# Two of four convolution blocks on GpSimd and ScalarE, and the threshold search's update on ScalarE

## The chip, the cores and the metric

The kernel runs on one core of a Trainium2 chip. A core has five engines with a queue of instructions each, worked off in order: TensorE (PE: matmuls, with weight loads as PEld), VectorE (DVE), ScalarE (ACT), GpSimd (POOL) and SyncE (SP, which issues the DMAs). They meet in two memories, SBUF and PSUM, and wait for one another through semaphores. The metric is the device time of one execution, in microseconds (us).

## The reference, cut to what matters

Two layers of a first block (`DEPTH = 2`), then a second block (a gated recurrence and an MLP), which the change doesn't touch. A layer of the first block, for 1024 tokens:

```python
p = h @ w_in[l]
u_val, u_gate, g_conv, c_q, c_kv, k_idx, w_idx, g_attn = jnp.split(p, offsets, axis=-1)
# conformer_conv: 512 channels, 31 taps, causal, depthwise
a = u_val * jax.nn.sigmoid(u_gate)
y = conv(a, conv_w) + conv_b
y_conv = (silu(layernorm(y, ln_g, ln_b)) @ w_pw2) * silu(g_conv)
# dsa_attention, for each block of 128 queries
score = einsum("bth,bths->bts", w_b, relu(einsum("bthd,bsd->bths", qi_b, k_idx)))
score = where(causal, score, -inf)
_, sel = lax.top_k(score, 256)
# ... attention over the selected keys, gated by silu(g_attn)
y = concatenate([y_conv, y_attn], -1) @ w_out[l]
x = x + gate * rmsnorm(y, g_post[l])
```

## The kernel before, in words

SBUF is cut into pages of 1024 float32 a partition; a buffer is a page (`pg`) or a list of pages. Products on TensorE are made from operands that are split in a high and a low part: ScalarE copies the high part (helper `split`, L264), VectorE subtracts it (L265). A scheduler orders the instructions of each engine at build time; the program gives it generators that yield after each unit of work, `weave` interleaves them by rates, and `prior` puts a generator's instructions forward or back in that order. At run time every queue is in order.

A layer's stages around the change, with their generators: `g_inputs` makes the convolution's four input blocks A[0] to A[3] (128 channels each by 1024 positions, even positions in the first half of a page, odd ones in the second; VectorE's L673 writes the halves). `g_latents` makes the latents of queries and keys (L801 on VectorE is their norm). `g_scores` runs over query blocks 2 to 4, then 5 to 7: matmuls L852, ScalarE's relu L854, VectorE's weighted sum L857 and L859, and at the end of each block GpSimd's causal mask L862 (`affine_select`). `g_gates` makes eight gate blocks on TensorE, evacuated by ScalarE (L689), with a weight split for each. `g_topk` finds, per query, the 256th largest score, bit by bit in two stages (15 and 16 bits): `top1` for query blocks 2 (VectorE, L921) and 3, 4 (ScalarE, L913), `top2` for 5, 6 (VectorE) and 7 (ScalarE). It begins with ScalarE's L893, which counts the scores above zero. For a ScalarE block, each bit is a count (a Sign with an accumulated sum), then three GpSimd operations on a column of 128 numbers (L916, L917, L919) that move the threshold `half`, which the next count reads.

`g_conv` computes the convolution of a block with three filters of half the length: a sum of the halves (L710), a scaled copy on ScalarE (L711), 15 + 30 + 2 = 47 fused taps on VectorE (L703: product with a column of weights plus the running sum, on 497 to 512 columns), and two copies of 15 columns (L726). It runs in the background of inputs, latents, scores and gates at priority -30, `top1` at -200. The layer norm of the four results (`g_norm_conv`) comes behind the search and the attention's preparation. Attention begins behind `top1`.

## Time and profile before

| | |
|---|---|
| runs before | 3029.22 and 3030.83 us, median 3030.02 |
| the profiled execution (span) | 3029.3 us |
| PE busy | 2906.8 us, 96% |
| DVE busy | 2229.9 us, 74% |
| ACT busy | 1679.8 us, 55% |
| POOL busy | 247.2 us, 8% |
| mean granted TensorE clock | 0.983 |

The profiled execution lasts 0.7 us less than the median. An engine's busy share is an average over the whole span. The page's part 2 cuts the span in 40 slices of 75.7 us and gives each engine's share there in tenths; PEclk is the granted TensorE clock (1.00 is the upper of its two levels, 2.4 GHz; a figure between is a mix with the lower, 1.2 GHz). Layer 0's conv inputs, latents and search lie in slices 2 to 6, layer 1's in slices 10 to 15. Every row read from it stands in its own section below.

### The profile page before, as it was taken

Reading aid. Unit: us, or ns where it says so; the run is one execution under the profiler, and the core shown is the slowest. Engines: PE = TensorE matmul, PEld = TensorE weight load, DVE = VectorE, ACT = ScalarE, POOL = GpSimd, SP = SyncE. Lnnn points to the kernel's source line nnn. Section 1 sums busy time; section 2 is a strip of 40 time slices with the busy share of each in tenths; the row PEclk is TensorE's granted clock in tenths of the full one; section 3 lists DMA queues with packets and bytes.
Section 4 is the critical chain, followed back from the end, with each engine's and each line's share of the span. In section 5 each row is a group of like instructions: output and inputs, shape, how many; then the busy total and the mean of one; then the engine's idle time right before and its main releaser. Section 6 shows DMA issues by size and latency. Waiting matters only on the chain.

```text
span 3029.3 us, 40735 instructions
## 1 busy us (share of the span) xinstructions
PE 2906.8 (96%) x15235; PEld 2362.8 (78%) x15235; DVE 2229.9 (74%) x4118; ACT 1679.8 (55%) x3032; POOL 247.2 (8%) x630
## 2 busy tenths in 40 slices
PE   9998787999999888999999999999999999999999
PEld 6877565778877665777888888888888888888887
DVE  5998899776988899756555667656666587776875
ACT  6248766737147866646444466555555654454454
POOL 0005511000005511000000000000000000000000
PEclk9999989999999989999999999999999999999999
DMA  8222102154101200133122211101013344456443
GB/s 276 63 40 63 42 18 77 48 193 149 39 18 42 63 19 18 36 112 118 49 62 62 79 35 36 56 29 56 29 37 122 103 143 153 151 201 238 153 146 111
DMA packets 218637, 264.14 MB, mean 87 GB/s; under 512 B 11504, under 2 KB 153543, under 8 KB 218439
## 3 DMA queue, kind: packets, MB, share of 16 engines
q1 hardware_dynamic: 218438, 261.54, 26.7%
q8 instruction: 119, 1.95, 0.3%
q14 instruction: 80, 0.65, 0.1%
HBM read 201.21 MB, written 60.29 MB: 86 GB/s over the span
## 4 chain that ended last, share of the span: by engine, by line
PE 58%; DVE 5%; POOL 2%; ACT 2%; DMA 1%; issue 1%; POOLq 0%; ACTq 0%
PE ps L269 15%; PE ps L271 15%; PE ps L270 15%; PE ps L331 5%; PE ps L1499 2%; DVE pg L921 2%; POOL consts L917 1%; PE ps L1164 1%; PE ps L1154 1%; POOL consts L919 1%; POOL consts L916 1%; DMA pg<-in_w_in_dram 1%; PE ps L1488 0%; DVE pg L1130 0%; PE ps L498 0%
## 5 line engine op out<-in xcount | busy, mean ns | idle before, releaser
L269 PE MATMUL ps<-pg,pg 128*128 128x512 f32 (+2 forms) x3080 | 1178.7, 384 | 15.1 <-DVE pg L265 4.2
L270 PE MATMUL ps<-pg,pg 128*128 128x512 f32 (+2 forms) x3080 | 1176.3, 383 | 0.0
L271 PE MATMUL ps<-pg,pg 128*128 128x512 f32 (+2 forms) x3080 | 1176.0, 382 | 0.0
L264 ACT ACTIVATE pg<-pg 128x512 fp32r<-128x512 f32 (+2 forms) x884 | 481.7, 591 | 527.7 <-PE ps L271 157.2
L269 PEld LDWEIGHTS ps<-pg,pg 128*128 128x128 f32 x3080 | 580.5, 189 | 132.9 <-DVE pg L265 10.1
L271 PEld LDWEIGHTS ps<-pg,pg 128*128 128x128 f32 x3080 | 580.6, 189 | 109.8 <-issue 3.7
L270 PEld LDWEIGHTS ps<-pg,pg 128*128 128x128 f32 x3080 | 580.8, 189 | 107.9 <-issue 3.5
L265 DVE TENSOR_TENSOR pg<-pg,pg 128x512 fp32r<-128x512 f32 (+2 forms) x884 | 528.2, 636 | 136.4 <-ACT pg L264 121.3
L278 POOL TENSOR_TENSOR consts<-consts 128x1 f32<-128x1 f32 x56 | 31.3, 559 | 2069.0 <-DVE consts L277 2069.0
L913 ACT ACTIVATE pg<-pg,consts 128x512 bf16<-128x512 uint16 (+5 forms) x186 | 166.8, 897 | 40.8 <-POOL consts L919 36.1
L703 DVE SCALAR_TENSOR_TENSOR pg<-pg,consts,pg 128x512 f32<-128x512 f32 (+15 forms) x256 | 176.9, 742 | 0.4
L331 PE MATMUL ps<-pg,pg 128*128 128x512 f32 x768 | 175.9, 389 | 0.0
L921 DVE TENSOR_SCALAR_CACHE_REDUCE pg<-pg,consts 128x384 bf16<-128x384 uint16 (+5 forms) x186 | 170.9, 919 | 2.3
L331 PEld LDWEIGHTS ps<-pg,pg 128*128 128x128 f32 x768 | 143.8, 188 | 29.6
L1138 ACT ACTIVATE pg<-pg,consts 128x256 f32<-128x256 f32 (+7 forms) x128 | 98.9, 774 | 70.2 <-DVE consts L1130 51.7
L1154 PE MATMUL ps<-consts,pg 128*128 128x128 f32 x576 | 107.7, 291 | 1.9 <-ACT pg L1160 1.1
L852 PE MATMUL ps<-pg,pg 128*128 128x512 f32 (+3 forms) x320 | 86.3, 370 | 14.7 <-DVE pg L844 9.4
L1164 PE MATMUL ps<-pg,pg 128*64 128x128 f32 x1152 | 92.5, 292 | 5.8 <-DVE pg L1147 1.7
L1116 PE MATMUL ps<-pg,pg 128*128 128x384 f32 (+5 forms) x192 | 79.4, 415 | 16.2 <-DVE consts L1130 7.9
L1160 ACT ACTIVATE pg<-ps 128x512 f32<-128x512 f32 (+1 forms) x112 | 57.8, 532 | 66.8 <-PE ps L1154 62.4
L917 POOL TENSOR_SCALAR consts<-consts 128x1 f32<-128x1 f32 x186 | 78.0, 419 | 179.1 <-ACT pg L913 173.5
L1164 PEld LDWEIGHTS ps<-pg,pg 128*64 128x64 f32 x1152 | 64.1, 141 | 35.1 <-issue 13.4
(350 smaller groups left out, 3810.7 us busy)
## 6 DMA issues: line engine op xcount, KB each, us to landing
pg<-in_w_in_dram SPq DMA_DIRECT2D x104, 512.0 KB
pg<-hidden SPq DMA_DIRECT2D x56, 512.0 KB
hidden<-pg SPq DMA_DIRECT2D x48, 512.0 KB
pg<-in_w_ada_dram SPq DMA_DIRECT2D x32, 512.0 KB
pg<-in_w_up_dram SPq DMA_DIRECT2D x32, 512.0 KB
pg<-in_w_down_dram SPq DMA_DIRECT2D x32, 512.0 KB
pg<-in_w_out_dram SPq DMA_DIRECT2D x24, 512.0 KB
x<-pg SPq DMA_DIRECT2D x24, 512.0 KB
```

What stands on the lines that cost most here:

```text
L264: self.nc.scalar.activation(hi, src, AF.Copy)
L265: self.nc.vector.tensor_sub(lo, src, hi.bitcast(F32))
L269: nc.tensor.matmul(ps, lhsT=wl, rhs=rh, start=first, stop=False)
L270: nc.tensor.matmul(ps, lhsT=wh, rhs=rl, start=False, stop=False)
L271: nc.tensor.matmul(ps, lhsT=wh, rhs=rh, start=False, stop=last)
L331: nc.tensor.matmul(ps, lhsT=w[z][k], rhs=act[y][k][:, a:b], start=k + n == 0, stop=3 * k + n == 3 * kt - 1)
L703: nc.vector.scalar_tensor_tensor(out, x[:, :512 - d], w, prev[:, d:], op0=OP.mult, op1=OP.add)
L913: nc.scalar.activation(junk_a(b), keys[b], AF.Sign, scale=-1.0, bias=col(tk["half"], b), accum_out=col(tk["cnt"], b))
L917: nc.gpsimd.tensor_scalar(col(tk["tm"], b), col(tk["cnt"], b), lim, -step, op0=OP.is_gt, op1=OP.mult)
L921: nc.vector.tensor_scalar(junk_d(b), keys[b], col(tk["cand"], b), None, op0=OP.is_ge, op1=OP.add, accum_out=col(tk["cnt"], b))
L1154: nc.tensor.transpose(pt[:, c:c + 128], Ps[hi][:, j * 128:j * 128 + 128], self.ident)
L1164: nc.tensor.matmul(uv[hi * 64:hi * 64 + 64], lhsT=V[j // 2][:, v:v + 64], rhs=th[:, jj * 256 + hi * 128:jj * 256 + hi * 128 + 128], start= ...
```

## The change

The blocks of the convolution are shared out: 0 and 1 stay on VectorE as fused taps, in one generator; 2 and 3 form a second one, `pconv`. For block 2 ScalarE makes each product into half a spare page (four halves in rotation) and GpSimd adds it to the running sum; for block 3 GpSimd makes the product too. Their first sum is on GpSimd as well. `pconv` has no priority offset; it runs along with the inputs and the latents and is drained before the scores are emitted. `Y` becomes a list that is filled by index.

In the search, ScalarE moves its own threshold: a Sign of the count plus a limit (`k2`, a column that VectorE presets), then an Identity that subtracts half a step times that sign. GpSimd has no part in the search any more. The start value and the limits are shifted to fit, and the column `hn` goes. All other lines of the diff remove comments.

```diff
+DVE_CONV, POOL_CONV = (0, 1), (2, 3)
...
-        A, Y, YA = [], [], []
+        A, Y, YA = [], [None] * 4, []
...
-        def g_conv():
+        def g_conv(blocks, split):
             cw, (g0, g1) = self.vec[f"conv_w{l}"], self.vec[f"conv_g{l}"]
-            add = nc.vector.tensor_add
+            add = nc.gpsimd.tensor_add if split else nc.vector.tensor_add
+            pp = self.pages(2) if split else []
+            prods = [pg[:, s] for pg in pp for s in halves]
 
             def tap(out, x, d, w, prev):
-                nc.vector.scalar_tensor_tensor(out, x[:, :512 - d], w, prev[:, d:], op0=OP.mult, op1=OP.add)
-            for j in range(4):
+                if split:
+                    q = self.ring("prods", prods)[:, :512 - d]
+                    if j == blocks[-1]:
+                        nc.gpsimd.tensor_scalar(q, x[:, :512 - d], w, None, op0=OP.mult)
+                    else:
+                        nc.scalar.activation(q, x[:, :512 - d], AF.Copy, scale=w)
+                    add(out, q, prev[:, d:])
+                else:
+                    nc.vector.scalar_tensor_tensor(out, x[:, :512 - d], w, prev[:, d:], op0=OP.mult, op1=OP.add)
+            for j in blocks:
...
                     for b in act:
                         nc.scalar.activation(junk_a(b), keys[b], AF.Sign, scale=-1.0, bias=col(tk["half"], b),
                                              accum_out=col(tk["cnt"], b))
-                        lim = col(tk["k2"], b) if limits else float(n_of[b] - 2 * TOPK)
-                        nc.gpsimd.tensor_scalar(col(tk["hn"], b), col(tk["half"], b), nxt, None, op0=OP.add)
-                        nc.gpsimd.tensor_scalar(col(tk["tm"], b), col(tk["cnt"], b), lim, -step, op0=OP.is_gt,
-                                                op1=OP.mult)
-                        nc.gpsimd.tensor_tensor(col(tk["half"], b), col(tk["tm"], b), col(tk["hn"], b), op=OP.add)
+                        nc.scalar.activation(col(tk["tm"], b), col(tk["cnt"], b), AF.Sign, bias=col(tk["k2"], b))
+                        nc.scalar.activation(col(tk["half"], b), col(tk["tm"], b), AF.Identity, scale=-0.5 * step,
+                                             bias=col(tk["half"], b))
...
-        conv = pr(g_conv(), 0)
+        conv, pconv = pr(g_conv(DVE_CONV, False), 0), g_conv(POOL_CONV, True)
...
-        weave((pr(g_inputs(), 11), 8), bg=[(more, RATES[l][8]), (conv, RATES[l][0])])
+        weave((pr(g_inputs(), 11), 8), bg=[(more, RATES[l][8]), (conv, RATES[l][0]), (pconv, 1.0)])
         drain(more)
         wq = idx_weights()
-        weave((pr(g_latents(), 9), 6), bg=[(conv, RATES[l][1])])
+        weave((pr(g_latents(), 9), 6), bg=[(conv, RATES[l][1]), (pconv, 6.0)])
+        drain(pconv)
```

The line numbers of the changed kernel are up to 14 higher: L862 is L875 there, L893 is L906, L913 is L928, L854 is L867, L264 is L265, L852 is L865. Its new lines are L710 (GpSimd's product), L712 (ScalarE's product), L713 (GpSimd's addition), L722 (the first sum), L930 and L931 (the threshold).

GpSimd's queue in layer 0, where the causal masks of the first score blocks stand. Before, they come first of all, and the search's columns follow:

```order
L278 TENSOR_TENSOR consts<-consts 128x1 x8
L862 AFFINE_SELECT pg_132_1342<-pg_132_1342 128x128
L862 AFFINE_SELECT pg_133_1343<-pg_133_1343 128x128
L862 AFFINE_SELECT pg_132_1342<-pg_132_1342 128x128
L916 TENSOR_SCALAR consts<-consts 128x1 x2
L917 TENSOR_SCALAR consts<-consts 128x1
L919 TENSOR_TENSOR consts<-consts 128x1
```

Now, the last rows of block 3's products and sums and what comes behind them (`pg_137`, `pg_138` hold the scores of query blocks 2 to 4, `pg_144` to `pg_146` those of 5 to 7):

```order
L710 TENSOR_SCALAR pg_69_582<-pg_95_833,consts 128x498 x2
L713 TENSOR_TENSOR pg_117_1149<-pg_69_582,pg_117_1149 128x498 x2
L710 TENSOR_SCALAR pg_68_581<-pg_95_833,consts 128x497 x2
L713 TENSOR_TENSOR pg_123_1380<-pg_68_581,pg_117_1149 128x497 x2
L875 AFFINE_SELECT pg_137_1520<-pg_137_1520 128x128
L875 AFFINE_SELECT pg_138_1521<-pg_138_1521 128x128
L875 AFFINE_SELECT pg_137_1520<-pg_137_1520 128x128
L875 AFFINE_SELECT pg_145_1817<-pg_145_1817 128x128
```

All 143 wide operations of the layer stand ahead of the first mask.

ScalarE's queue at the start of `top1`'s first stage in layer 0 (counts, relu of scores, gate evacuations and weight splits). Before:

```order
L893 ACTIVATE pg_146_1687,consts<-pg_132_1342,consts 128x640
L854 ACTIVATE pg_143_1670<-ps 128x1024
L689 ACTIVATE pg_152_1731<-ps 128x512
L913 ACTIVATE pg_146_1687,consts<-pg_148_1689,consts 128x512
L689 ACTIVATE pg_152_1731<-ps 128x512
L843 ACTIVATE pg_145_1672<-ps 128x384
L854 ACTIVATE pg_143_1670<-ps 128x896
L843 ACTIVATE pg_145_1672<-ps 128x384
L854 ACTIVATE pg_144_1671<-ps 128x896
L913 ACTIVATE pg_146_1687,consts<-pg_147_1688,consts 128x640
L854 ACTIVATE pg_144_1671<-ps 128x768
L913 ACTIVATE pg_146_1687,consts<-pg_148_1689,consts 128x512
```

Now:

```order
L867 ACTIVATE pg_148_1820<-ps 128x896
L906 ACTIVATE pg_150_1836,consts<-pg_137_1520,consts 128x640
L867 ACTIVATE pg_148_1820<-ps 128x768
L928 ACTIVATE pg_150_1836,consts<-pg_152_1838,consts 128x512
L930 ACTIVATE consts<-consts 128x1
L928 ACTIVATE pg_150_1836,consts<-pg_151_1837,consts 128x640
L931 ACTIVATE consts<-consts 128x1
L930 ACTIVATE consts<-consts 128x1
L928 ACTIVATE pg_150_1836,consts<-pg_152_1838,consts 128x512
```

From there all 30 counts of the stage and their 60 column operations follow one another without any other work; the next relu (L867) comes behind them, and eight rows further the split of the next gate weights, `L265 ACTIVATE pg_154_1873<-pg_153_1872 128x1024`. In layer 1 such a piece has 26 counts and 52 column operations.

TensorE's queue near that place in layer 0, the last score units and the gate product that needs these weights (`pg_154`, and `pg_155`, which VectorE's L266 makes from it):

```order
L865 MATMUL ps<-pg_109_1023,pg_149_1821 128x512 x2
L865 MATMUL ps<-pg_110_1024,pg_149_1821 128x512 x2
L865 MATMUL ps<-pg_109_1023,pg_149_1821 128x448 x2
L865 MATMUL ps<-pg_110_1024,pg_149_1821 128x448 x2
L270 MATMUL ps<-pg_42_288,pg_155_1874 128x512
L271 MATMUL ps<-pg_50_296,pg_154_1873 128x512
L272 MATMUL ps<-pg_42_288,pg_154_1873 128x512
```

The product's weights come from the split behind ScalarE's piece of counts.

## Rows read from the trace of the kernel before

**Rows 1.** The page, part 1: busy us, share and instructions of each engine.
```profile
PE 2906.8 (96%) x15235; PEld 2362.8 (78%) x15235; DVE 2229.9 (74%) x4118; ACT 1679.8 (55%) x3032; POOL 247.2 (8%) x630
```

**Rows 2.** Stretches: length, busy PE, PEld, DVE, ACT, POOL, granted clock, DMA share, GB/s.
```profile
111.00:232.00 121.00, 120.09 (x551) 97.43 (x549) 117.47 (x215) 44.77 (x77) 0.80 (x2) 1.00 0.21 40
232.00:354.00 122.00, 100.40 (x416) 78.57 (x416) 98.92 (x237) 96.12 (x196) 82.86 (x190) 0.93 0.19 58
354.00:400.00 46.00, 35.87 (x135) 25.04 (x134) 44.73 (x102) 38.04 (x69) 7.93 (x33) 0.93 0.08 25
...
925.00:1046.00 121.00, 105.07 (x441) 81.69 (x439) 104.95 (x259) 100.90 (x210) 84.00 (x190) 0.96 0.19 60
1046.00:1100.00 54.00, 46.49 (x197) 35.34 (x198) 51.67 (x128) 39.92 (x78) 10.35 (x43) 0.78 0.08 24
```

**Rows 3.** Stretches, VectorE's taps (L703) alone: length, busy, count, clock; layer 0.
```profile
232.00:300.00 68.00, 16.36 (x22) 0.97 0.19 57
300.00:350.00 50.00, 18.29 (x25) 0.89 0.14 46
```

**Rows 4.** Timeline (start, duration, us): block 2's input complete, masks, search; both layers.
```profile
109.56 1.09 DVE L673 SCALAR_TENSOR_TENSOR pg<-pg,ps 128x512 f32<-128x512 f32 x1
...
231.20 1.00 POOL L862 TENSOR_SCALAR_AFFINE_SELECT pg<-pg 128x128 f32<-128x128 f32 x2 [203.47 <-DVE pg L859]
...
232.51 0.62 ACT L893 ACTIVATE pg<-pg,consts 128x384 bf16<-128x384 int16 x1
...
806.68 1.12 DVE L673 SCALAR_TENSOR_TENSOR pg<-pg,ps 128x512 f32<-128x512 f32 x1 [1.63 <-PE ps L271]
...
924.95 0.63 ACT L893 ACTIVATE pg<-pg,consts 128x384 bf16<-128x384 int16 x1
```

**Rows 5.** VectorE: taps (ns min/median/max); 111 to 232: L859, then L265; L801.
```profile
L703 DVE SCALAR_TENSOR_TENSOR pg<-pg,consts,pg x256: 718/744/762, 103.4 to 1021.6; 128x498 f32<-128x498 f32 x10, 128x510 f32<-128x510 f32 x9, 128x504 f32<-128x504 f32 x9, 128x502 f32<-128x502 f32 x9
...
111.00:232.00 121.00, 14.38 (x21) 1.00 0.21 40
...
111.00:232.00 121.00, 7.49 (x8) 1.00 0.21 40
...
L801 DVE SCALAR_TENSOR_TENSOR pg<-pg,consts,pg 128x512 f32<-128x512 f32 x4 | 2.8, 739 | 0.0
```

**Rows 6.** GpSimd's operations in the whole program: ns min/median/max.
```profile
L862 POOL TENSOR_SCALAR_AFFINE_SELECT pg<-pg x12: 290/296/1324, 231.2 to 1011.5; 128x128 f32<-128x128 f32 x12
...
L917 POOL TENSOR_SCALAR consts<-consts x186: 211/300/1312, 237.5 to 1191.0; 128x1 f32<-128x1 f32 x186
...
L919 POOL TENSOR_TENSOR consts<-consts x186: 190/192/1249, 237.8 to 1191.3; 128x1 f32<-128x1 f32 x186
```

**Rows 7.** Timeline of VectorE and GpSimd, layer 0's search: start and duration in us.
```profile
267.98 1.15 DVE L859 SCALAR_TENSOR_TENSOR pg<-pg,consts,pg 128x896 f32<-128x896 f32 x1
...
272.48 0.61 DVE L921 TENSOR_SCALAR_CACHE_REDUCE pg<-pg,consts 128x384 bf16<-128x384 int16 x1
...
268.04 1.18 POOL L917 TENSOR_SCALAR consts<-consts 128x1 f32<-128x1 f32 x1
...
272.61 0.22 POOL L917 TENSOR_SCALAR consts<-consts 128x1 f32<-128x1 f32 x1
```

**Rows 8.** ScalarE: scaled copy and 15 columns (ns min/median/max); L913's 30 counts, busy.
```profile
L546 ACT ACTIVATE pg<-pg,consts x2: 725/726/726, 37.2 to 44.3; 128x512 f32<-128x512 f32 x2
...
232.00:296.00 64.00, 25.96 (x60) 0.97 0.19 56
...
L726 ACT ACTIVATE pg<-pg x16: 201/218/220, 125.5 to 1025.9; 128x15 f32<-128x15 f32 x16
```

**Rows 9.** Waits in layer 0 (0 to 640 us): total, times, longest, in us.
```profile
ACT pg L913 <- POOL consts L919: 17.7, 24, 1.5
...
PE ps L302 <- ACT pg L294: 12.6, 1, 12.6
```

More of the change, by code (lines that the diff above doesn't have):

```diff
@@ L429, in rest @@
             self.widx = self.const(8, 8)
-            self.tk = {nm: self.const(8) for nm in ("cnt", "tm", "cand", "hi", "k2", "g", "r", "half", "hn", "neg")}
+            self.tk = {nm: self.const(8) for nm in ("cnt", "tm", "cand", "hi", "k2", "g", "r", "half", "neg")}
             self.tki = {nm: self.const(8, dt=I32) for nm in ("xor", "hi", "lo")}
@@ L721, in g_conv @@
                         yield
-                y = self.page()
-                Y.append(y)
+                y = Y[j] = self.page()
                 for yc, (zc, x, g) in zip((y[:, 0::2], y[:, 1::2]), lines):
@@ L728, in g_conv @@
                 yield
+            if split:
+                self.free(pp)
             self.dump(f"y{l}", Y)
@@ L902, in g_topk @@
             nc.vector.tensor_scalar(tk["half"][:, na], tk["neg"][:, na], -32768.0, 16383.5, op0=OP.mult, op1=OP.add)
+            for b in act:
+                nc.vector.memset(col(tk["k2"], b), 2.0 * TOPK - n_of[b] - 0.5)
             for b in bs[::-1]:
@@ L933, in stage @@
                     yield
-                nc.vector.tensor_scalar(tk["cand"][:, na], tk["half"][:, na], 0.5, None, op0=OP.add)
+                nc.vector.tensor_copy(tk["cand"][:, na], tk["half"][:, na])
             yield from stage(KH, 14, False)
@@ L948, in g_topk @@
                 else:
-                    nc.vector.tensor_scalar(col(tk["k2"], b), col(tk["g"], b), 2.0 * n_of[b] - 2 * TOPK, None,
-                                            op0=OP.add)
+                    nc.vector.tensor_scalar(col(tk["k2"], b), col(tk["g"], b), -1.0, 2.0 * TOPK - 2.0 * n_of[b] - 0.5,
+                                            op0=OP.mult, op1=OP.add)
             nc.vector.memset(tk["cand"][:, nb], 32768.0)
```

## The prediction

> **What bounds the kernel now.** The page's first part comes first: TensorE (PE) is busy 96% of the span, VectorE (DVE) 74%, ScalarE (ACT) 55%, GpSimd (POOL) 8% [rows 1]. So a change to DVE, ACT and POOL can only act where PE waits. The table of stretches shows where that is in the two attention layers [rows 2]. In 111 to 232 us, where the index latents and the first scores are made, PE is busy 120.09 of 121 us: nothing can be gained there, although DVE is full too (117.47). In 232 to 354 and 354 to 400, the threshold search, PE is busy 100.40 + 35.87 of 168 us and so idle 31.7. In layer 1 the same work (925 to 1100) has it busy 105.07 + 46.49 of 175 us, idle 23.4. The two together, 55 us or 1.8%, are the most that the change could win in these places. The granted TensorE clock is below full there (0.93, 0.78) against 1.00 in the stretches before.
>
> Next I asked what starts the search. Its first ScalarE instruction (L893) begins at 232.51 us and in layer 1 at 924.95 [rows 4], right behind POOL's affine_selects (L862), for which POOL has sat idle 203.5 us: it has no other work before [rows 4].
>
> **What changes on VectorE.** Blocks 2 and 3 leave: 2 x 47 taps at 0.74 us [rows 5] and two additions, about 71 us per layer. In layer 0, 47 of them ran behind 232 us, 22 + 25 [rows 3], and shared DVE with the search there. This frees DVE, but what it frees counts only if DVE is what PE waits for, and POOL must now do the work first.
>
> **What changes on GpSimd.** POOL gets, per layer, 96 additions of two pages' halves (94 taps and two sums) and 47 products, 143 instructions of 497 to 512 columns. All of them stand ahead of the six affine_selects in its queue, as the POOL order rows show. It loses 279 column updates (L916, L917, L919).
>
> No row shows a wide POOL operation, so I bound its price. A 128x1 one takes 192 ns (L919's median); the 128x128 affine_select, which reads one input, 296 ns [rows 6]. That is 104/127 = 0.82 ns a column; a 505-column operation with one input would then take 0.192 + 0.41 = 0.61 us. If the two inputs of an addition are read one after the other, it takes 0.192 + 0.83 = 1.02 us. Sum: 96 x 1.02 + 47 x 0.61 = 127 us. Lower end: every one of the 143 at the one-input price, with the smaller slope from L917's shortest (211 ns): 85/127 = 0.67 ns a column, 0.52 us each with 0.19 fixed, 74 us. Upper end: an addition costs three passes, 1.43 us, 166 us in all. I take 127 because the nearest row is the 128x128 operation, the only one with more than a column.
>
> **The lock between GpSimd and VectorE.** The timeline shows POOL's tiny operations stretched to the end of whichever two-input operation DVE is in [rows 7]: L917 began at 268.04 and took 1.18 us, ending with DVE's L859 (267.98 + 1.15); the same L917 took 0.22 during the one-input L921 at 272.48. So POOL's work and DVE's two-input work from pages don't overlap. Whether a wide POOL operation holds DVE up in the same way no row shows, since the taps, 0.762 us at most, are no longer beside the tiny ones [rows 5]. For the sum it doesn't matter who yields: their times add.
>
> By the Trainium skill (SBUF — State Buffer, Who interferes with whom) a VectorE instruction with two SBUF inputs contends with a GpSimd instruction that reads SBUF, and the one that comes second blocks fully; the rows agree for POOL's side, 1.18 us against 0.22. The Trainium skill (Perfetto Trace Analysis, Optimizing Scalar/DVE Operations) speaks against this change: offloading between those two engines might not help.
>
> From the moment block 2's input is complete (109.56 + 1.09 = 110.7 us [rows 4]), DVE has in its new order, up to the end of the first score group, 67 taps of blocks 0 and 1 and a sum (68 x 0.744 = 50.6 us), L859 in 111 to 232 (14.4), L265 (7.5) and L801 (2.8) [rows 5]: 75 us with two page inputs. So POOL ends at 110.7 + 127 + 75 = 313 us. The affine_selects follow it, and the search starts about 80 us later than 232.5. ScalarE's 47 products (0.726 us each, by the one 128x512 operation with a column scale [rows 8]: 34 us) are faster than the additions that consume them. With four half-page slots ACT then goes at POOL's pace, which holds the few instructions between the products, but that lies inside the same 202 us. I cost it at nothing as long as POOL is what ends last.
>
> **ScalarE in the search.** Each of the 93 counts per layer is now followed by two 128x1 operations (0.218 us each, by L726's 128x15) in place of three POOL ones. ACT gains 186 x 0.218 = 41 us per layer and loses its waits for POOL, 17.7 us in layer 0 [rows 9]. What matters more is what is queued. By the ACT order rows the first 30 counts and their 60 updates now stand in one piece, ahead of the score evacuations and of the split of the next gate weights, where before they alternated. PE's next gate product (the PE order rows) needs that split. The piece takes 26 us for the 30 counts with the reads of their sums [rows 8], 60 x 0.218 = 13 us, and about 6 us more for the three counts ahead of it (L893, 0.62 the first) and the split: 45 us. In layer 1, by 26 counts and 52 updates, 22.5 + 11.3 + 5 = 39 us.
>
> **The sum.** Layer 0: POOL ends at 313, PE gets its weights at 358. Of the 136.3 us of PE work that lay between 232 and 400, about 8 (the score units ahead of the stall) are done by then. 128 are left, plus 13 of idle time that the change doesn't touch (the 12.6 us wait of L302 [rows 9], taken for both layers): 358 + 141 = 499 against 400, +99. Layer 1: 806.68 + 1.12 + 202 = 1010, + 39 = 1049. PE's 151.6 - 8 + 13 = 157 brings 1206 against 1100, +106. Together +205 us on the profiled 3029.3, which is 0.7 below the median of 3030.02: **3235 us**.
>
> **Rivals.**
> *No lock on wide operations* (POOL and DVE overlap; for it: the taps never grew; against it: rows 7). POOL ends at 110.7 + 127 = 238, PE gets weights at 283, ends at 424, +24; layer 1 935 + 39 + 157 = 1131, +31. Time 3085.
>
> *The other side: not slower.* If the 143 operations, waits included, average under 122/143 = 0.85 us (mine: 202/143 = 1.41), POOL ends by 232.5 and delays nothing. At the lower price without lock it ends at 185. Then the bunched counts are all that is left: 232.5 + 45 + 141 = 418, +18, and 925 + 39 + 157 = 1121, +21: 3069. If in addition PE's score units fill the bunch, the freed DVE time and POOL's lost waits shorten the search, and all idle time but L302's goes: -(31.7 - 12.6) - (23.4 - 12.6) = -30, 3000. For it: POOL's ops are short when nothing blocks them (0.22). Against it: DVE is full in this stretch, so the pair is rarely free.
>
> *Worse.* Three passes an addition with lock: 39 us more per layer, 3313; also if the granted clock, 0.78 in the last search stretch, falls further behind the long stall.
>
> **Numbers.** Lock as forecast 0.62, from 3129 (lower price, 53 us less per layer) to 3313. No lock 0.20, around 3085, from 3069 to 3130 (additions with three passes). Other side 0.12, 3000 to 3069. Worse than 3313 0.06. The range 3068 to 3315 leaves out about 0.18. A measurement of this kernel tells about 2% from no change (2969 to 3091). Faster by more 0.03; within 0.19 (the rest of the other side and half of no lock); slower 0.78.
>
> **What would show it.** In the changed trace: POOL busy near 200 us from 111 us on, its additions either long (they include the wait) or DVE's taps longer than 0.77 us; the affine_selects at 310 us or later; ACT waiting for POOL before the first count; then PE idle in one piece of over 80 us, ended by the weight split behind the counts. The forecast is wrong if the affine_selects come before 250 us, if additions take under 0.6 us beside two-input taps, or if PE's gate product starts while counts are still running.

## The result and the profile after

The changed kernel takes 3392.78 us (median of two runs, 3392.53 and 3393.02) against 3030.02: 1.1197 times as long, 95% interval 1.1176 to 1.1218. That is 363 us more, where 205 were forecast, and outside the range that ended at 3315. The direction was right. The size was not, and one step of the mechanism behind it failed.

The first lines of the page after the change: busy time of each engine, then GpSimd, the granted clock and TensorE in 40 slices (here 84.8 us each).

```profile
span 3390.7 us, 40634 instructions
PE 2938.2 (87%) x15235; PEld 2383.6 (70%) x15235; DVE 2218.0 (65%) x3932; ACT 1836.4 (54%) x3518; POOL 445.4 (13%) x358
PE   9841578889996084888999999999999999999999
POOL 0698000000039900000010000000000000000000
PEclk9875788989998597999999999999999999999999
```

TensorE's work is nearly the same (2938 us busy against 2906.8 [rows 1]), and its instructions are as many. Of the 361 us between the two profiled executions 330 are idle time of TensorE and 31 busy time, at a mean granted clock of 0.931 against 0.983. The idle time lies in two places, one per layer: slices 3 to 5 and 13 to 16, counted from 1. GpSimd's 9, 8 and 9, 9 stand in slices 3, 4 and 13, 14. VectorE has lost 12 us of 2229.9 in all, although 188 of 376 taps left it. So its other taps got longer.

Layer 0 in stretches (from:to, length, busy PE, PEld, DVE, ACT, POOL with counts, granted clock, DMA share, GB/s); the first two answer to 111 to 232 and 232 to 354 in [rows 2].

```profile
111.00:232.00 121.00, 71.19 (x302) 57.88 (x300) 113.73 (x108) 45.95 (x70) 114.40 (x75) 0.79 0.04 12
232.00:354.00 122.00, 41.86 (x159) 31.24 (x160) 12.21 (x24) 22.21 (x33) 91.09 (x69) 0.65 0.05 11
...
232.00:280.00 48.00, 12.59 (x44) 9.90 (x44) 2.07 (x7) 0.00 (x0) 48.00 (x37) 0.61 0.00 0
280.00:330.00 50.00, 6.19 (x15) 3.65 (x16) 1.38 (x2) 7.15 (x12) 43.09 (x33) 0.52 0.02 7
330.00:380.00 50.00, 48.89 (x228) 38.63 (x227) 26.91 (x42) 30.33 (x52) 0.99 (x2) 1.00 0.34 52
380.00:430.00 50.00, 6.18 (x23) 4.02 (x21) 29.07 (x114) 46.59 (x151) 0.29 (x1) 0.59 0.06 17
```

Between 232 and 280 us GpSimd works almost alone: ScalarE has not one instruction, VectorE seven, TensorE is busy 12.59 of 48 us. From 330 to 380 TensorE is full again (48.89 of 50), and only then, from 380 to 430, comes the idle time of the bunched search that the prediction had placed right behind GpSimd's end. A whole block of TensorE's work, the latents and the first scores, has slid behind GpSimd.

The waits of layer 0 say by what (engine and line waited for: total, times, longest, us; the last line is the wait in 380 to 430 us):

```profile
ACT pg L737 <- POOL pg L713: 109.4, 4, 103.9
DVE pg L715 <- POOL pg L713: 88.7, 1, 88.7
...
PE ps L303 <- ACT pg L809: 77.6, 1, 77.6
...
PE ps L865 <- ACT pg L867: 40.7, 2, 40.0
```

And the timeline of ScalarE, VectorE and GpSimd around that place (start, duration, us; idle time before, and what ended it):

```profile
316.70 0.22 ACT L737 ACTIVATE pg<-pg 128x15 f32<-128x15 f32 x1 [103.90 <-POOL pg L713]
...
323.12 1.15 ACT L809 ACTIVATE pg<-pg 128x512 f32<-128x512 f32 x2 [5.18 <-POOL pg L713]
...
323.12 1.38 DVE L715 SCALAR_TENSOR_TENSOR pg<-pg,consts,pg 128x497 f32<-128x497 f32 x2 [88.66 <-POOL pg L713]
...
320.69 2.40 POOL L713 TENSOR_TENSOR pg<-pg,pg 128x497 f32<-128x497 f32 x2
378.74 0.99 POOL L875 TENSOR_SCALAR_AFFINE_SELECT pg<-pg 128x128 f32<-128x128 f32 x2 [55.66 <-DVE pg L872]
```

L737 copies the 15 edge columns of block 3's result, 0.22 us of work. It waits for GpSimd's last sums for 103.9 us, and in ScalarE's queue it stands ahead of L809, the squares for the latents' norm; TensorE's L303, the norm's sum over the rows, waits 77.6 us for those. L809 has a second wait for GpSimd, and it ends last: the squares go to the page that was GpSimd's working page of block 3, so they begin at 323.12 us, 5.2 us behind the copies. The copies alone could have been moved without starting them earlier. VectorE stops at its last taps of block 1: they write to a page that was one of `pconv`'s product pages. GpSimd ends at 323.1 us; the masks wait another 55.7 us for scores that had not been begun. The search starts at 379.6 us (232.5 before [rows 4]).

GpSimd's and VectorE's prices (ns min/median/max; answers to [rows 5, 6]), and the new column operations on ScalarE:

```profile
L713 POOL TENSOR_TENSOR pg<-pg,pg x188: 1054/1276/2243, 115.2 to 1192.0; 128x511 f32<-128x511 f32 x12, 128x510 f32<-128x510 f32 x12, 128x509 f32<-128x509 f32 x12, 128x508 f32<-128x508 f32 x12
...
L710 POOL TENSOR_SCALAR pg<-pg,consts x94: 1524/1550/2537, 184.2 to 1189.3; 128x511 f32<-128x511 f32 x6, 128x510 f32<-128x510 f32 x6, 128x509 f32<-128x509 f32 x6, 128x508 f32<-128x508 f32 x6
...
L715 DVE SCALAR_TENSOR_TENSOR pg<-pg,consts,pg x128: 703/1150/1777, 101.9 to 1188.9; 128x512 f32<-128x512 f32 x8, 128x511 f32<-128x511 f32 x8, 128x510 f32<-128x510 f32 x8, 128x509 f32<-128x509 f32 x8
...
L930 ACT ACTIVATE consts<-consts x186: 277/283/311, 385.8 to 1553.7; 128x1 f32<-128x1 f32 x186
```

Both engines pay for being busy together: a tap of this form has a median of 1.150 us against 0.744 before. ScalarE isn't the cause of that: seven taps of the changed kernel up to 330 us that ran beside a busy ScalarE and an idle GpSimd took 0.730 to 0.747 us.

Milestones show that the two layers lose alike. In layer 0, from before to after: search start 232.5 to 379.6 us (+147.1), first product of the attention 390.5 to 562.6 (+172.1). Layer 1 begins 180 us late (its block 2's input, 806.68 to 986.87); from there the search start is 146 us later (924.95 to 1251.2) and the attention's first product 172 (1074.4 to 1426.2). So each layer loses about 172 us on the way to the attention: 90.6 until GpSimd's end (323.1 against 232.5), 56.5 for latents and scores behind it, 25 in the search. About 19 of the 363 us fall elsewhere and are not accounted for one by one.

One line of the section on the kernel before needs a correction: of the two searches it is `top2` whose instructions are put back by 200; `top1` has no offset. No term of the sum used it.

### The profile page after: what moved, and what is told of

Same layout as the page of the kernel before. It is cut to its first block, busy times and chain, and to the rows that moved or that the text cites. A ratio compares the mean times of both kernels' runs of the same rounds, so it can differ in the third digit from the quotient of the medians.

```text
span 3390.7 us, 40634 instructions
## 1 busy us (share of the span) xinstructions
PE 2938.2 (87%) x15235; PEld 2383.6 (70%) x15235; DVE 2218.0 (65%) x3932; ACT 1836.4 (54%) x3518; POOL 445.4 (13%) x358
## 4 chain that ended last, share of the span: by engine, by line
PE 66%; DVE 11%; POOL 10%; ACT 7%; issue 4%; DMA 2%; SPq 0%; POOLq 0%; ACTq 0%; DVEq 0%
PE ps L270 16%; PE ps L272 16%; PE ps L271 16%; POOL pg L713 5%; PE ps L332 5%; POOL pg L710 4%; DVE pg L934 4%; ACT pg L928 2%; PE ps L1513 2%; PE ps L1178 2%; PE ps L1168 2%; PE ps L865 1%; DVE pg L1144 1%; DVE pg L872 1%; DMA pg<-in_w_in_dram 1%
## 5 line engine op out<-in xcount | busy, mean ns | idle before, releaser
L265 ACT ACTIVATE pg<-pg 128x512 fp32r<-128x512 f32 (+2 forms) x884 | 481.3, 591 | 502.8 <-PE ps L272 140.2
L270 PEld LDWEIGHTS ps<-pg,pg 128*128 128x128 f32 x3080 | 586.6, 191 | 214.6 <-DVE pg L266 34.7
L271 PEld LDWEIGHTS ps<-pg,pg 128*128 128x128 f32 x3080 | 586.7, 190 | 110.7 <-issue 3.9
L272 PEld LDWEIGHTS ps<-pg,pg 128*128 128x128 f32 x3080 | 585.7, 190 | 108.8 <-issue 1.0
L266 DVE TENSOR_TENSOR pg<-pg,pg 128x512 fp32r<-128x512 f32 (+2 forms) x884 | 535.4, 643 | 163.7 <-ACT pg L265 149.1
L715 DVE SCALAR_TENSOR_TENSOR pg<-pg,consts,pg 128x512 f32<-128x512 f32 (+15 forms) x128 | 141.7, 1176 | 185.4 <-POOL pg L713 185.3
L713 POOL TENSOR_TENSOR pg<-pg,pg 128x511 f32<-128x511 f32 (+15 forms) x188 | 250.6, 1349 | 5.7 <-ACT pg L712 3.1
L303 PE MATMUL ps<-pg,consts 128*128 128x512 f32 x56 | 31.6, 670 | 172.2 <-ACT pg L809 172.2
L928 ACT ACTIVATE pg<-pg,consts 128x512 bf16<-128x512 uint16 (+5 forms) x186 | 165.9, 892 | 3.6 <-DVE pg L919 2.3
L332 PEld LDWEIGHTS ps<-pg,pg 128*128 128x128 f32 x768 | 143.9, 188 | 29.6
L865 PE MATMUL ps<-pg,pg 128*128 128x512 f32 (+3 forms) x320 | 91.6, 392 | 79.3 <-ACT pg L867 45.2
L710 POOL TENSOR_SCALAR pg<-pg,consts 128x511 f32<-128x511 f32 (+15 forms) x94 | 153.1, 1634 | 0.3
L303 PEld LDWEIGHTS ps<-pg,consts 128*128 128x128 f32 x56 | 10.9, 209 | 178.7 <-ACT pg L809 173.6
L865 PEld LDWEIGHTS ps<-pg,pg 128*128 128x128 f32 x320 | 60.9, 204 | 97.1 <-ACT pg L867 53.2
L872 DVE SCALAR_TENSOR_TENSOR pg<-pg,consts,pg 128x640 f32<-128x640 f32 (+5 forms) x84 | 78.0, 948 | 70.7 <-ACT pg L867 70.2
```

The lines of the kernel that those rows point to most:

```text
L265: self.nc.scalar.activation(hi, src, AF.Copy)
L266: self.nc.vector.tensor_sub(lo, src, hi.bitcast(F32))
L270: nc.tensor.matmul(ps, lhsT=wl, rhs=rh, start=first, stop=False)
L271: nc.tensor.matmul(ps, lhsT=wh, rhs=rl, start=False, stop=False)
L272: nc.tensor.matmul(ps, lhsT=wh, rhs=rh, start=False, stop=last)
L332: nc.tensor.matmul(ps, lhsT=w[z][k], rhs=act[y][k][:, a:b], start=k + n == 0, stop=3 * k + n == 3 * kt - 1)
```

## The experiments

Each time is the median of four executions, beside the kernel before (3028.4 to 3030.9 us there), unless it says otherwise.

**Each half alone: e1_conv_only, e2_search_only.** The first takes the changed convolution with the old three GpSimd operations per count, the second the old convolution with the new update:

```diff
 # e1_conv_only, against the changed kernel
-nc.scalar.activation(col(tk["tm"], b), col(tk["cnt"], b), AF.Sign, bias=col(tk["k2"], b))
-nc.scalar.activation(col(tk["half"], b), col(tk["tm"], b), AF.Identity, scale=-0.5 * step, bias=col(tk["half"], b))
+nc.gpsimd.tensor_scalar(col(tk["hn"], b), col(tk["half"], b), nxt, None, op0=OP.add)
+nc.gpsimd.tensor_scalar(col(tk["tm"], b), col(tk["cnt"], b), lim, -step, op0=OP.is_gt, op1=OP.mult)
+nc.gpsimd.tensor_tensor(col(tk["half"], b), col(tk["tm"], b), col(tk["hn"], b), op=OP.add)
 # e2_search_only, against the kernel before: the reverse
```

> The convolution as in the changed kernel (two blocks off VectorE), the search's threshold updates on GpSimd as before. In the changed trace the search of layer 0 begins at 379.6 us against 232.5 before (+147), and from there to the attention's first product takes 183 us against 158 (+25). Theory (the convolution's place in GpSimd's queue makes the loss, the update on ScalarE adds only its own 60 x 0.283 us in the bunched stage): the search still begins at about 380 us, the bunch gets 10 to 17 us shorter per layer, time 3340 to 3375. Rival (half or more of the loss is the search's): 3210 or less.

3343.04 us, ratio 1.1036 (1.102 to 1.1053): +314 us. The search begins at 379.6 us, the same as in the changed kernel. The convolution makes the larger loss. Its stretch 380 to 430 us, and TensorE's wait in it:

```profile
380.00:430.00 50.00, 4.26 (x20) 3.03 (x18) 33.45 (x134) 43.59 (x101) 28.63 (x129) 0.57 0.06 18
...
PE ps L865 <- ACT pg L867: 45.1, 2, 44.4
```

So TensorE stands still behind the counts of layer 0 with the old update too, 44.4 us against 40.0: in this kernel's queue the 30 counts of the first stage also follow one another in one piece. In layer 0 the bunch comes with the convolution's change, and the update on ScalarE adds 10 us (173 us from the search's start to the attention's first product, 183 in the changed kernel). In layer 1 it adds 36 (139 against 175).

> The convolution as before on VectorE, the threshold update on ScalarE. Theory: the counts of the first stage stay mixed with score evacuations and weight splits, so there is no bunch; ScalarE gains 186 x 0.283 = 53 us per layer and loses 18 us of waits, of which PE sees 5 to 25 per layer: 3040 to 3080. Rival (the update on ScalarE paces the search and PE waits for all of it): 3110 or more. Rival (the lost waits for GpSimd pay): 3015 or less.

3101.88 us, ratio 1.0243 (1.0227 to 1.0258): +73 us, between the first two expectations, and the piece of counts is there after all. In this kernel's queue 75 instructions of the search follow one another (25 counts, 50 updates). Its stretch 260 to 296 us:

```profile
260.00:296.00 36.00, 19.50 (x80) 15.93 (x79) 19.59 (x58) 35.94 (x110) 0.00 (x0) 0.76 0.09 29
```

TensorE's waits from 232 to 354 us in it:

```profile
PE ps L852 <- DVE pg L844: 29.3, 2, 28.1
PE ps L852 <- ACT pg L854: 17.6, 3, 16.5
```

ScalarE is full (35.94 of 36 us) with counts, TensorE waits 28.1 us for score operands and 16.5 for a relu (3.8 and 3.0 us in all before), and the attention's first product slips from 390.5 to 416.3 us. So my expectation that the counts stay mixed was wrong: the bunch doesn't need the convolution's change, and by e1 not the new update either. The two halves add to 314 + 73 = 387, 24 more than the 363 of both.

**The two waits taken away: e3_unblock.**

```diff
-                    nc.scalar.activation(yc[:, :15], zc[:, :15], AF.Copy)
-                self.free(A[j], z)
+                    if split:
+                        nc.gpsimd.tensor_copy(yc[:, :15], zc[:, :15])
...
+                if split and j == blocks[-1]:
+                    held.extend([A[j], z])
...
-                self.free(pp)
+                held.extend(pp)
...
         sp = self.pages(2)
+        self.free(held)
```

> The changed kernel with two waits for GpSimd's last block taken away: the 15-column edge copies of blocks 2 and 3 on GpSimd instead of ScalarE, and the pages of block 3 and of the products handed out again only after the first scores' pages are taken. Theory (ScalarE's edge copy and VectorE's write to a product page hold the latents and with them the first scores, 57 us of work behind GpSimd's end at 323): latents and the first score group run beside GpSimd, GpSimd ends 10 to 25 us later because of the added two-input work, the search begins at 335 to 365 instead of 379.6, time 3290 to 3350. Rival (what the scores' VectorE work costs GpSimd through the shared port gives it all back): search at 375 or later, 3380 or more.

3320.74 us, ratio 1.0962 (1.0943 to 1.098): 72 us less than the changed kernel, as the theory had it. The mechanism is seen in the stretch where ScalarE and VectorE had stood nearly still:

```profile
232.00:280.00 48.00, 39.74 (x161) 28.78 (x162) 30.59 (x41) 21.62 (x38) 48.00 (x33) 0.88 0.24 32
```

TensorE is busy 39.74 of 48 us there (12.59 in the changed kernel), and GpSimd's masks follow its last sum at once, at 331.8 us. The search itself starts at 376.6, later than expected: in this kernel's queue both score groups stand ahead of the first count, and the second group's pages wait for GpSimd (ScalarE's relu 32.2 us, and TensorE 29.0 behind that). So the waits are shown as the cause of a part, 36 us per layer, not of all 56.5.

**Only block 2: e4_one_block, e11_one_block_old.** Block 3 goes back to VectorE, so GpSimd keeps 48 additions per layer; the second kernel has the old search as well.

```diff
-DVE_CONV, POOL_CONV = (0, 1), (2, 3)
+DVE_CONV, POOL_CONV = (0, 1, 3), (2,)
...
-                    if j == blocks[-1]:
+                    if j == 3:
```

> Only block 2 leaves VectorE (products on ScalarE, additions on GpSimd), block 3 is back on VectorE; search as in the changed kernel. GpSimd then has 48 additions per layer in place of 143 operations. Theory: 48 x 1.3 us from 112 us on end at about 175, before the latents' norm and far before the masks at 231, so the search begins within 8 us of 232.5; what is left is the update on ScalarE: 3030 to 3085. Rival (VectorE's taps, stretched from 0.74 to 1.15 us beside GpSimd, delay latents and scores as well): search at 250 or later, 3110 or more.

3176.7 us, ratio 1.0488 (1.0472 to 1.0503): the rival. GpSimd is idle from 186 us on, long before any mask, and yet the search begins at 271.5 us instead of 232.5. Stretches of e4_one_block:

```profile
111.00:160.00 49.00, 34.11 (x147) 28.20 (x146) 48.93 (x44) 26.46 (x38) 45.39 (x32) 0.79 0.06 17
...
200.00:232.00 32.00, 20.55 (x73) 13.77 (x72) 28.22 (x48) 11.48 (x16) 0.00 (x0) 0.79 0.02 9
```

TensorE's waits in it from 100 to 280 us:

```profile
PE ps L270 <- DVE pg L674: 14.9, 1, 14.9
PE ps L800 <- DVE consts L801: 11.5, 1, 11.5
PE ps L270 <- DVE consts L474: 6.8, 1, 6.8
```

In 111 to 160 us VectorE is full in both kernels (48.93, and 48.83 before), but it finishes 44 instructions in place of 95. TensorE, which was busy 120.09 of 121 us in 111 to 232 before [rows 2], waits 33 us there for VectorE's inputs and norms: 14.9 + 11.5 + 6.8. This is the lock of the two engines seen from the other side. GpSimd was not late for anyone; it made VectorE late.

> Block 2 alone on ScalarE and GpSimd as in e4_one_block (3177), the search's updates on GpSimd as before. Theory (the losses add: 72 us for the search, 75 for one block of convolution beside the inputs and latents, where VectorE's two-input work is slowed): 3090 to 3120, and the search of layer 0 begins at about 270 us as in e4_one_block. Rival (one block costs only together with the search change): 3060 or less.

3110.09 us, ratio 1.0267 (1.0252 to 1.0282): +82 us for one block without the search change, and 67 less than with it. Here the losses of search (73 alone) and convolution nearly add.

**What GpSimd's products cost: e5_act_products.** Block 3's products go to ScalarE too.

```diff
-                    if j == blocks[-1]:
+                    if False:
                         nc.gpsimd.tensor_scalar(q, x[:, :512 - d], w, None, op0=OP.mult)
```

> The changed kernel with block 3's 47 products on ScalarE too, so that GpSimd keeps only the 96 additions per layer. In the changed kernel GpSimd's products took 1.52 us each with no contender, 78.8 us in layer 0, in the middle of the chain that PE waits for. Theory (GpSimd's serial work in front of the latents sets the time): GpSimd ends at 235 to 255 instead of 323, the search of layer 0 begins at 295 to 320 instead of 379.6, time 3220 to 3270. Rival (ScalarE, which then paces 94 products at 0.72 us with four half pages, becomes the bound and blocks the latents' evacuations behind it): gain under 60 us, 3330 or more.

3245.14 us, ratio 1.071 (1.0694 to 1.0726): 148 us less than the changed kernel. The 94 products took 153.1 us of GpSimd's time in it, so nearly all of their time had cost. In layer 0 GpSimd ends at 255.9 us (224.55 + 31.31), 67 us earlier, and the search begins at 326.3, 53 earlier but a little later than expected; another 24 us go in the search itself, whose counts stand in another order in this kernel's queue. In layer 1 the search begins 72 us earlier, counted from the layer's inputs.

```profile
224.55 31.31 POOL L713 TENSOR_TENSOR pg<-pg,pg 128x508 f32<-128x508 f32 x23
309.48 0.99 POOL L875 TENSOR_SCALAR_AFFINE_SELECT pg<-pg 128x128 f32<-128x128 f32 x2 [53.62 <-DVE pg L872]
```

**Without the contender: e6_alone** (a single execution, so no interval). VectorE's taps of blocks 0 and 1 are left out but for 5 of 47.

```diff
-                    nc.vector.scalar_tensor_tensor(out, x[:, :512 - d], w, prev[:, d:], op0=OP.mult, op1=OP.add)
+                    if d in (0, 15):
+                        nc.vector.scalar_tensor_tensor(out, x[:, :512 - d], w, prev[:, d:], op0=OP.mult, op1=OP.add)
...
-                        nc.gpsimd.tensor_scalar(q, x[:, :512 - d], w, None, op0=OP.mult)
+                        nc.gpsimd.tensor_scalar(q, x[:, :512 - d], 0.5 if l else w, None, op0=OP.mult)
```

> The changed kernel, leaving out 42 of the 47 taps of each of blocks 0 and 1 on VectorE, so that GpSimd has hardly a contender for its port; in layer 1 GpSimd's products multiply by a number instead of a column of weights. Theory (lock): GpSimd's additions of block 2 fall from a mean of 1.34 us to 1.05 to 1.10, PE is busy over 44 of 49 us in 111 to 160 (34.1 in the changed kernel), and GpSimd ends at 280 to 300 instead of 323. Rival (1.34 us is GpSimd's own price, no lock): additions stay above 1.25 us and GpSimd ends at 315 or later. On the price of the product: if the column is what costs 1.52 us, it falls below 1.1 in layer 1; if it is the operation, it stays at 1.5.

GpSimd's additions while it works on block 2 (busy, mean ns), of the changed kernel, 112 to 181 us:

```profile
L713 POOL TENSOR_TENSOR pg<-pg,pg 128x511 f32<-128x511 f32 (+15 forms) x42 | 60.4, 1461 | 2.8 <-ACT pg L712 1.5
```

and of e6_alone, 112 to 167.5 us:

```profile
L713 POOL TENSOR_TENSOR pg<-pg,pg 128x511 f32<-128x511 f32 (+15 forms) x44 | 52.5, 1215 | 2.8 <-ACT pg L712 1.5
```

A stretch of e6_alone, to be read beside the same one of e4_one_block:

```profile
111.00:160.00 49.00, 45.27 (x205) 37.36 (x204) 10.70 (x8) 31.71 (x48) 46.21 (x39) 0.98 0.06 16
```

And the two forms of its product (ns min/median/max; above by a column, in layer 0, below by a number, in layer 1):

```profile
L710 POOL TENSOR_SCALAR pg<-pg,consts x47: 1530/1551/2613, 168.2 to 296.1; 128x511 f32<-128x511 f32 x3, 128x510 f32<-128x510 f32 x3, 128x509 f32<-128x509 f32 x3, 128x508 f32<-128x508 f32 x3
L710 POOL TENSOR_SCALAR pg<-pg x47: 1462/1482/2460, 1018.9 to 1142.1; 128x511 f32<-128x511 f32 x3, 128x510 f32<-128x510 f32 x3, 128x509 f32<-128x509 f32 x3, 128x508 f32<-128x508 f32 x3
```

The additions fall from 1.461 to 1.215 us, short of the 1.05 to 1.10 expected, and below the 1.25 of the rival: there is a lock, and it costs GpSimd about 0.25 us an addition, not the length of a tap. (Some two-input work is left on VectorE here, so 0.25 is a lower bound.) TensorE gets its 45.27 of 49 us. GpSimd ends at 300.0 (323.1), just within what was expected. The product is slow by itself: 1.482 us with a number, 1.551 with a column. In all, 3346.61 us: 46 less than the changed kernel, for a VectorE with almost no convolution. So what VectorE's taps do to GpSimd is a small part of the whole loss as long as GpSimd's chain is that long.

**Behind the masks: e7_late, e9_late_free.** Block 3 alone goes to GpSimd, and only after all scores are emitted. e9 also puts the edge copies on GpSimd and holds block 3's pages until the gates are done.

```diff
+DVE_CONV, POOL_CONV = (0, 1, 2), (3,)
...
         weave((pr(g_scores(wq, 1), 4), 24), ...)
+        drain(pconv)
         norm_keys()
 # e9_late_free also
+                        nc.gpsimd.tensor_copy(yc[:, :15], zc[:, :15])
...
-        self.free(hT)
+        self.free(hT, held)
```

> Blocks 0 to 2 on VectorE, block 3 alone on GpSimd (products and additions), emitted behind all scores, so that GpSimd's queue has the first masks ahead of it; search as in the changed kernel. VectorE is rid of the 47 taps that shared the search stage with it. Theory (the place in the queue made the loss, not the work): the search begins within 5 us of 232.5, the result lies at or below the search change alone (3102): 3050 to 3110. Rival (the lock with VectorE's work in the search stage, and GpSimd's end after 430, cost as much as the taps did or more): 3130 or more. Rival (the freed VectorE pays in full): 3028 or less.

3310.24 us, ratio 1.0929 (1.091 to 1.0947): 208 us worse than the search change alone, though the search begins at 232.8. The loss is a wait of the same kind in another place. Waits from 233 to 500 us:

```profile
POOL pg L722 <- PE ps L270: 112.2, 1, 112.2
...
PE ps L303 <- ACT pg L295: 103.6, 1, 103.6
ACT pg L737 <- POOL pg L713: 95.1, 2, 91.2
```

GpSimd can't begin until 346 us, as its working page is one that TensorE still reads. ScalarE's edge copies then hold the keys' norm, and TensorE stands still for 103.6 us.

> Block 3 alone on GpSimd, behind the first masks in its queue, as in e7_late (3310), but with what ScalarE waited for there taken away: block 3's 15-column edge copies on GpSimd instead of ScalarE (they held the keys' norm and PE for 91 to 104 us in layer 0), and its pages handed out again only after the gates. Theory (the waits of in-order engines behind GpSimd's chain make the loss, GpSimd's work by itself costs little): close to the search change alone (3102), 3080 to 3140. Rival (the shared port, with VectorE's two-input work of the search stage beside GpSimd, or the late end of block 3 before the layer norm, keeps most of the loss): 3200 or more.

3273.55 us, ratio 1.0803 (1.0785 to 1.0821): 37 us better, and not the 3080 to 3140 of the theory. The wait has only changed its name. From 380 to 520 us:

```profile
PE ps L270 <- DVE pg L266: 77.3, 3, 75.1
ACT pg L265 <- DMA pg<-toep: 77.0, 2, 76.3
...
SPq L1085 <- POOL pg L715: 91.5, 2, 90.4
```

The table of near biases is loaded into one of the pages that GpSimd gives back at 484 us; its DMA has to wait (90.4 us in SyncE's queue for GpSimd's addition, L715 in this kernel), ScalarE's split waits for it, and TensorE for that. I had not freed the path of the GpSimd chain, only moved what hangs on it. What GpSimd's work would cost in a kernel with pages to spare was not shown.

**What the search's update costs: e8_three, e10_one_op,** both against e2_search_only, with three and with one column operation per count in place of two.

```diff
 # e8_three
-nc.scalar.activation(col(tk["half"], b), col(tk["tm"], b), AF.Identity, scale=-0.5 * step, bias=col(tk["half"], b))
+nc.scalar.activation(col(tk["tm"], b), col(tk["tm"], b), AF.Identity, scale=-0.5 * step)
+nc.scalar.activation(col(tk["half"], b), col(tk["tm"], b), AF.Identity, scale=1.0, bias=col(tk["half"], b))
 # e10_one_op
-nc.scalar.activation(col(tk["tm"], b), col(tk["cnt"], b), AF.Sign, bias=col(tk["k2"], b))
-nc.scalar.activation(col(tk["half"], b), col(tk["tm"], b), AF.Identity, scale=-0.5 * step, bias=col(tk["half"], b))
+nc.scalar.activation(col(tk["half"], b), col(tk["cnt"], b), AF.Identity, scale=-0.5 * step / n_of[b], bias=col(tk["half"], b))
```

> The kernel with the search change alone (3102), with a third 128x1 operation on ScalarE per count (the step and the sum apart): 93 x 0.283 = 26 us more of ScalarE per layer. Theory (what the search change costs is ScalarE's time in the search, of which PE saw 36 of 53 us per layer): 3125 to 3160. Rival (the cost comes from another order of the queues, not from ScalarE's time): 3095 to 3112.

3103.89 us, ratio 1.0243 (1.0228 to 1.0259), the same as with two. The third operation, which has no column as its bias, took 0.195 us (row L918 in the last section), so it added 18 us per layer and not 26. The rival's number, but not by its reason: the scheduler mixed this kernel's counts again, the attention's first product comes at 393.7 us (390.5 before, 416.3 with two operations), and the time is lost later. In 500 to 560 us, where VectorE and ScalarE still work at the second search, TensorE is busy 28.11 of 60 us (51.43 before).

```profile
500.00:560.00 60.00, 28.11 (x112) 14.40 (x112) 50.60 (x121) 38.69 (x91) 0.00 (x0) 0.66 0.25 75
```

> The search change alone, leaving out the Sign, so that one 128x1 operation per count is left on ScalarE (the thresholds that it finds are not the reference's; the number of instructions per bit doesn't depend on them). In its queue no piece of counts without other work is longer than 10 instructions (75 in the search change alone, none over 12 in e8_three's first layer). Theory (what e8_three lost without such pieces, it lost by ScalarE's time): 52 us less of it per layer than e8_three, time 3030 to 3065. Rival (a ScalarE that counts without waiting for GpSimd holds up its other work by order alone): 3085 or more. Rival (the 18 us of lost waits per layer pay): 3015 or less.

3041.26 us, ratio 1.004 (1.0025 to 1.0055): as the theory had it. Without bunches and with one operation, 13 us are left of the loss; with three, 73. So ScalarE's own time counts, and with two operations the bunches were added to it or took its place; how the 73 us of two operations divide between the two is not settled. The lost waits for GpSimd, 17.7 us in layer 0 [rows 9], brought no net gain in any of the three.

**All repairs: e12_all_three.** All products on ScalarE (as e5), copies and pages as in e3, the old search (as e1).

> Both blocks still leave VectorE, but with three things put right at once: all products on ScalarE, the edge copies on GpSimd with the pages held as in e3_unblock, and the search's updates on GpSimd as before. Theory (the separate losses add up: 148 us of GpSimd's products, 72 of the search, some of the 72 that the two waits cost, fewer now because GpSimd's chain is shorter): 3130 to 3185, and what remains over the kernel before is VectorE and GpSimd slowing each other in the latents. Rival (the parts hide one another, so that the sum of the repairs brings the kernel back to before or below): 3060 or less.

3205.7 us, ratio 1.0584 (1.0563 to 1.0606), 20 us above what was expected and far from the rival. GpSimd's chain now ends at 259.8 us, the masks of the first scores come at 306.4, and 176 us remain over the kernel before: two blocks beside the latents, with VectorE at half its pace, cost about twice what one does (82). VectorE's taps in 112 to 260 us, and TensorE's longest waits from 100 to 450:

```profile
L717 DVE SCALAR_TENSOR_TENSOR pg<-pg,consts,pg 128x506 f32<-128x506 f32 (+15 forms) x52 | 78.7, 1584 | 0.1
...
PE ps L808 <- DVE consts L809: 34.3, 1, 34.3
PE ps L270 <- DVE pg L266: 16.4, 2, 8.2
```

The single repairs gained 148 (e5), 72 (e3) and 50 us (e1), 270 in all; together they gained 187. So they overlap, and the theory's adding didn't hold here. No run here beat the kernel before.

## Why the prediction was wrong

- **GpSimd's end: nearly right by luck, by two errors that met.** Forecast 313 us, measured 323.1. Additions alone take 1.05 to 1.27 us (forecast 1.02). The products take 1.55 instead of 0.61: 47 x 0.94 = 44 us more. The lock takes less than the full sum of times that I set, 75 us: taken away but for a little, it gave 23 us (e6). The one-input slope of the mask operation was no guide to the product's price.
- **The step that failed: "The affine_selects follow it", and of what ScalarE holds meanwhile, "I cost it at nothing as long as POOL is what ends last".** I let latents and first scores run beside GpSimd. In fact ScalarE's edge copies of block 3 and pages that change hands put them behind it, 56.5 us per layer. e3, which takes these waits away, gives back 36 of that per layer; there a page of GpSimd's holds the second score group instead, and the remaining 20 were not shown apart. The rows for that were in the queues before any run: L737 stands ahead of L809 in ScalarE's order. I had looked at GpSimd's queue, asked who waits for its last instruction there (the masks), and not who else waits for it.
- **VectorE was not just a contender but a bound.** "For the sum it doesn't matter who yields: their times add" failed twice. GpSimd paid 23 us of the 75 (e6), and VectorE's delay reaches TensorE directly, as e4 shows with 39 us of later search and GpSimd long idle.
- **The bunched search: right in size, not in its cause.** 45 us forecast from GpSimd's end to the weights. In the trace TensorE is busy 6.18 of 50 us in 380 to 430, with one wait of 40.0 us behind L867, and the search as a whole takes 25 us longer, against the 18 that the 3069 of a rival had for the bunch. But the bunch doesn't hang on the new update: e1 has a wait of 44.4 us there without it. The column operations took 0.283 us, not 0.218.
- **Layers.** 99 and 106 us were forecast. Measured to the attention's first product: 172 and 172. The 73 of layer 0 are 10 (GpSimd's end) + 56.5 (latents and scores) + 6.5 (search).
- **Signs named beforehand:** GpSimd busy near 200 us from 111 on (205.5 in 111 to 354), masks after 310, taps over 0.77 us: all seen. "ACT waiting for POOL before the first count" was seen too, but at L737 and for the latents, not at the count. "PE idle in one piece of over 80 us, ended by the weight split" wasn't: it came as two pieces with 50 full microseconds of latents and scores between.

## What to carry to other kernels

Work given to an idle engine isn't free because the engine was idle: price it per instruction on that engine by a run, and see whether it slows the engine that it is taken from. Then list everybody who waits for its last result, the small copies and the pages that it gives back included: here a 0.22 us copy and the reused pages of one chain stopped three engines for 78 to 104 us. And before taking work off an engine, look whether TensorE waits for it at all; here it was busy 120.09 of 121 us in the stretch where VectorE was full.

## What the runs showed of the hardware

- A product of 497 to 512 float32 columns by a column of weights takes 1.55 us on GpSimd, 1.48 by a number, while an addition of two such operands takes 1.05 to 1.27: the operation with one input is the slower one. ScalarE does the same product in 0.717 us, VectorE product and sum together in 0.744.
- The addition has two prices without a contender (changed kernel, 236 to 316 us): 1.06 to 1.08 us at 511, 510, 507, 506, 503, 502, 499 and 498 columns, 1.23 to 1.27 at 512, 509, 508, 505, 504, 501, 500 and 497. With 512 - d columns the running sum is read and written d columns into its half page, so the price goes with d: low where d leaves 1 or 2 when divided by 4, high where it leaves 0 or 3. Why was not tested.

```profile
L713 POOL TENSOR_TENSOR pg<-pg,pg 128x503 f32<-128x503 f32 x2 | 2.1, 1068 | 0.0
L713 POOL TENSOR_TENSOR pg<-pg,pg 128x501 f32<-128x501 f32 x2 | 2.4, 1226 | 0.0
```

- With GpSimd adding and VectorE in its taps at the same time, five of each went by in 7.6 and 8.0 us (rows below, from the changed kernel): 1.52 and 1.59 us each, in step, where additions of these widths (499 to 503 columns) take 1.13 on average and the taps 0.744 alone, 1.87 one after the other. So the two overlap, but by 0.3 us a pair only. The product with one input is held up too: 1.97 us on average beside taps (15 of them in 184 to 233 us), 1.55 alone.

```profile
127.71 7.61 POOL L713 TENSOR_TENSOR pg<-pg,pg 128x503 f32<-128x503 f32 x5
...
126.41 7.97 DVE L715 SCALAR_TENSOR_TENSOR pg<-pg,consts,pg 128x503 f32<-128x503 f32 x5
```

By the Trainium skill (SBUF — State Buffer, Who interferes with whom) the contended pair of ports is an exclusive lock. The trace agrees that both are held up, VectorE too, which the kernel before couldn't show. It differs in that the lock can't last for the whole of both instructions: 1.59 us a pair instead of 1.87.

- A 128x1 operation on ScalarE with a column as its bias takes 0.277 to 0.311 us, against 0.201 to 0.220 for the 128x15 copies that stood for it [rows 8]. It is the column and not the place in a chain that costs: in e8_three the operation without one (L918) took 0.195 us between its neighbours with one (L919: 0.288).

```profile
L918 ACT ACTIVATE consts<-consts x186: 185/195/231, 238.3 to 1262.4; 128x1 f32<-128x1 f32 x186
L919 ACT ACTIVATE consts<-consts x186: 276/288/327, 238.5 to 1262.6; 128x1 f32<-128x1 f32 x186
```

- TensorE's granted clock was 0.52 in 280 to 330 us, where it was busy 6.19 of 50, and 1.00 in 330 to 380, where it was busy 48.89. 0.5 is the lower of its two levels.
